# Gated DeltaNet stage of a two-layer hybrid block: exp(G) by broadcast DMA, chunk-major keys and queries, output norm with tokens on partitions, and the inverse merges of both directions in one job

## Chip, cores and metric

One core of one Trainium2 chip runs the whole program. The metric is the device time in microseconds of one execution, from the median of several runs.

## The reference, cut to what matters

The model has two layers. Each layer normalises the latent stream (1024 tokens, width 1024) and a context prefix (256 tokens), projects both through one input matrix, feeds three head groups, and projects their joined outputs back. The groups are windowed attention (8 heads of 64), a bidirectional gated DeltaNet (4 heads of 128) and a bidirectional RG-LRU. The change is almost entirely in the DeltaNet group. In the reference, for one direction:

```python
G = jnp.cumsum(g, axis=-1)
kk = jnp.einsum("bnhid,bnhjd->bnhij", k, k)
lmat = jnp.where(strict, beta[..., :, None] * jnp.exp(diff) * kk, 0.0)
a_mat = lmat + jnp.eye(C)
gam = jnp.exp(G)
w = triangular_solve(a_mat, (beta * gam)[..., None] * k)
u = triangular_solve(a_mat, beta[..., None] * v)
kdec = jnp.exp(G[..., -1:] - G)[..., None] * k
...
u_n = u_n - jnp.einsum("bhcd,bhde->bhce", w_n, s)
s_new = gl_n * s + jnp.einsum("bhcd,bhce->bhde", kdec_n, u_n)
o = einsum("bhcd,bhde->bhce", gam * q, s) + einsum("bhij,bhje->bhie", aqk, u_n)
...
rms_norm(o_forward + o_backward, norm_w) * silu(z)
```

## The kernel before

All 1280 tokens of a layer lie feature-major (features on partitions) through the projections. The matrices of the two projections are split into a high and a low part in a rounded fp32 format, so each product is three matmuls of 128x512 or 128x256. Everything else on TensorE is plain fp32, where one matmul call is two matmul records in the trace.

The program has no loops on the chip. Python threads (generators) yield operations with an engine, a cost, the buffers read and the buffers written; the class `Driver` takes the ready operation with the lowest start time plus priority and emits it. The order on every engine is thus fixed by the costs that the code states, by the tables of priorities `PR` (layer 0) and `PR1` (layer 1), and by the lists `ORDER` and `ORDER1`, which say in which order the 34 column tiles of the input projection go through TensorE. Engines run their instructions in that order.

A layer has these stages, which overlap where data allow it. `phase_a`: the input projection (`inproj`), the convolutions and norms of keys and queries (`kq_thread`, which spills them to the DRAM tensor `kqd`), the decays (`col_thread`, which leaves the running sums G in `col["G"]` and, as rows, in the tile `GR`), the matrices of each chunk (`prep_thread`, to the DRAM tensors `Md` and `Ad`), and the inverses of the 32x32 diagonal blocks (`inv_thread`, to `XXd`). `phase_b`: the recurrence. `phase_c`: attention over blocks of 128 tokens. `stage3`: the output projection and the residual.

The recurrence works in 10 chunks of 128 tokens and in two directions. For each direction and chunk `gjob` builds the 128x128 inverse of all four heads from its 32x32 diagonal blocks: `expand` on POOL (L1661), two matmul stages on 32x32 tiles of the array (`q32`, 16 records; `r32`, 24 records) and two on 64x64 tiles (`q64`, `r64`, 8 records each), with copies out of PSUM between them (L1676, L1677, L1693, L1695, L1707, L1718, L1720). `gside` loads and scales the chunk's operands: four matmuls `gb` against one-hot columns (`sel`) spread the rows of `GR` over the partitions, ACT takes the exponential (L1623), POOL multiplies keys and queries by it (L1628). `gchain` is the recurrence itself, one thread a direction: four matmuls `ks`, a subtraction on DVE (L1748), four matmuls `um`, a copy (ACT L1758, or DVE L1761), four matmuls `sm`, four state updates on DVE (L1779), and eight matmuls `om` for the output, which comes out feature-major and is summed over the directions (L1797, L1799). `gprep` lets two jobs of each direction be in flight. `gfinish` norms two chunks at a time (nine pairs in all: five in layer 0, four in layer 1): squares on ACT (L1824), one 128x512 fp32 matmul with a matrix of ones for each chunk, logarithm and exponential on ACT (L1827, L1829), a product on DVE (L1831, twice) and one with the gate (L1833).

Most DMAs are issued by SP. Attention's loads of keys (`kstd`, 8 loads) and of queries (`qstd`, 18 loads of 512 KB, into two buffers) are issued by POOL, because `q_att` is "gq".

Of the kernel before, what the change touches and what calls it, by code (L numbers as in the profile page):

```python
# [221 lines left out]
class Driver:  # L222


    def __init__(self):
# [7 lines left out]
        self.PR = {"att": -2.43, "att_k": -1.14, "att_q": 0.4, "atth": -0.23, "ba": 0.43, "evac": 0.48,  # L233
                   "gchain": 0.91, "gdn_q": -0.6, "gdn_v": 0.32, "gfin": -1.1, "gprep": 0.91, "gside": 1.4,
                   "inproj": 1.2, "inv": 0.64, "lru_x": -0.32, "lru_z": -1.34, "modlate": -1.04, "modload":
                   -3.18, "norm": 0.04, "normA": -2.69, "normB": -0.47, "normC": -0.78, "oproj": 0.17, "osplit":
                   -1.96, "prep": 0.37, "ptev": -0.1, "resid": -0.85, "rope": 1.9, "score": -0.06, "wprep":
                   -0.37, "z": -0.63}
        self.ops, self.late = [], False
        self.PR1 = {"att": -2.33, "att_k": -1.36, "att_q": -0.73, "atth": 0.31, "ba": 1.51, "evac": 0.09,  # L240
                    "gchain": 1.44, "gdn_q": -1.55, "gdn_v": 0.24, "gfin": 0.31, "gprep": 0.73, "gside": 0.54,
                    "inproj": 1.06, "inv": 0.21, "lru_x": -0.54, "lru_z": -1.12, "normA": 1.74, "normB": 2.27,
                    "normC": 6.51, "oproj": -0.33, "osplit": -2.98, "prep": -0.71, "ptev": -1.57, "resid":
                    -16.03, "rope": 5.61, "score": -0.18, "wprep": -0.07, "z": -0.78}
        self.margin, self.setpen, self.tilepen = 2.72, 1.1, 0.26
        self.cap = {"pe": 0.25, "dve": 0.3, "act": 0.33, "pool": 0.73}
# [165 lines left out]
def c_dve(n):  # L412
    return 0.07 + n / 960.0
# [14 lines left out]
def c_pool1(n):  # L428
    return 0.19 + n * 0.00097
# [99 lines left out]
class Build:  # L529
    def __init__(self, nc, tc, A, out):  # L530
# [8 lines left out]
        self.q_inv, self.q_att, self.e_rope, self.e_kq, self.e_lru = "sp", "gq", "dve", "dve", "dve"  # L539
# [445 lines left out]
    def params(self):  # L985
# [37 lines left out]
        for k in "aeflr":  # L1023
            for l in range(2):
                yield ops[k, l]

    ORDER = ("gdn_k0", "gdn_q1", "gdn_q0", "gdn_k1", "gdn_q2", "gdn_v1", "gdn_k3", "gdn_k2", "gdn_z3", "gdn_q3",
             "lru_z1", "lru_x0", "lru_x1", "lru_z0", "lru_z2", "lru_z3", "gdn_v2", "gdn_v3", "lru_x3", "gdn_v0",
             "lru_x2", "gdn_z1", "att_q3", "att_v0", "gdn_z2", "att_q0", "att_q2", "att_q1", "att_k0", "gdn_z0",
             "att_z3", "att_z0", "att_z2", "att_z1")  # L1030
    ORDER1 = ("gdn_q0", "lru_z3", "gdn_q1", "gdn_k0", "gdn_k1", "gdn_v2", "gdn_k2", "gdn_k3", "gdn_q2",
              "gdn_q3", "lru_x3", "lru_z1", "lru_x2", "lru_z0", "gdn_v3", "lru_x1", "gdn_z3", "att_v0",
              "gdn_v1", "gdn_z2", "lru_z2", "att_k0", "att_q1", "gdn_v0", "lru_x0", "att_q2", "att_z1",
              "att_q3", "att_q0", "gdn_z1", "att_z0", "gdn_z0", "att_z2", "att_z3")
# [70 lines left out]
    def zones(self):  # L1105
# [5 lines left out]
        for l in range(2):  # L1111
# [16 lines left out]
                              s=[z.slots("s", 2, [512]) for _ in range(2)], fz=z.slots("fz", 2, [1024]), osum=z.slots("osum", 10, [512]))  # L1128
# [117 lines left out]
    def col_thread(self, C):  # L1246
# [42 lines left out]
        for c0_, nck in ((0, 4), (4, 4), (8, 2)):  # L1289
# [9 lines left out]
            yield ("dve", c_dve(n), lambda: nc.vector.tensor_sub(self.GR.t[32:40, sl], pr.t[:8, :n], self.GR.t[0:8, sl].bitcast(F32)), [pr, self.GR], [self.GR])  # L1299
            pr.free()  # L1300
        C["evs"]["col"].fire()
# [280 lines left out]
    def phase_b(self, l):  # L1582
# [9 lines left out]
        for d in range(2):  # L1592
            drv.spawn(self.gprep(C, d, order[d], pre), 0.0, f"gprep{d}", self.ev(l, "gprep", d))
            drv.spawn(self.gchain(C, d, order[d]), -0.3, f"gchain{d}", self.ev(l, "gchain", d))
# [46 lines left out]
    def gjob(self, C, d, c):  # L1641
        nc, col = self.nc, self.col
        J = {}
# [610 lines left out]
```

## Time and profile before

| what | value |
|---|---|
| time, median of 3 runs | 2046.93 us (2044.83 to 2052.85) |
| time of the profiled execution | 2044.17 us |
| its span, first to last instruction | 2042.4 us |
| TensorE matmul busy | 1954.8 us, 96% |
| TensorE weight loads busy | 1551.9 us, 76% |
| VectorE (DVE) busy | 1310.4 us, 64% |
| ScalarE (ACT) busy | 1099.2 us, 54% |
| GpSimd (POOL) busy | 451.1 us, 22% |
| mean granted TensorE clock | 0.988 of full |
| moved by DMA | 327.45 MB |

The span is what the profile covers; the device time of the same execution is 1.8 us longer. The matmul row counts a matmul from its start to a modelled end, and matmuls overlap, so the distance from one start to the next is the better measure of what one costs when TensorE is full. PE is TensorE, PEld its weight loads, SP the engine that issues most DMAs.

### The profile page before, as it was taken

The page shows a single profiled execution, that of the slowest core. Times are in us where ns is not written, and L with a number is a line of the kernel's source. Part 1 is how long each engine was busy: PE and PEld are TensorE (multiplying, and loading weights), DVE is VectorE, ACT ScalarE, POOL GpSimd, SP SyncE. Part 2 cuts the span into 40 slices and gives each one's busy share as a digit, 9 for nine tenths or more (in the row PEclk, how much of TensorE's full clock was granted, in tenths as well). Part 3 has the DMA queues.
Part 4 walks back from the last instruction along what each step waited for, and adds up shares of the span by engine and source line. Part 5 has one row for each costly group of instructions (what it writes and reads, how often), then busy time and mean ns, then how long its engine had stood idle before and what let it go on. Part 6 is the DMA issues. An engine that isn't in the chain of part 4 may idle for free.

```text
span 2042.4 us, 35176 instructions
## 1 busy us (share of the span) xinstructions
PE 1954.8 (96%) x13138; PEld 1551.9 (76%) x13138; DVE 1310.4 (64%) x2529; ACT 1099.2 (54%) x1942; POOL 451.1 (22%) x630
## 2 busy tenths in 40 slices
PE   5899999999999989999999999999999999999997
PEld 2588888778888976667788787777777888766785
DVE  4867698997733455764624668888978434676523
ACT  3567667666533445565423576667657334566432
POOL 2302210000064740011322110200000676200233
PEclk8999999999999999999999999999999999999998
DMA  8125644424566796765633145643354776734644
GB/s 296 35 97 175 179 142 121 122 76 152 186 215 220 220 275 194 228 171 151 211 116 104 62 158 145 186 129 99 95 179 147 219 210 211 202 83 125 209 139 129
DMA packets 319082, 327.45 MB, mean 160 GB/s; under 512 B 62448, under 2 KB 240576, under 8 KB 318912
## 3 DMA queue, kind: packets, MB, share of 16 engines
q1 hardware_dynamic: 299040, 310.53, 49.0%
q0 software_dynamic: 19872, 14.68, 3.3%
q8 instruction: 103, 1.69, 0.4%
q14 instruction: 67, 0.55, 0.1%
HBM read 225.10 MB, written 94.79 MB: 157 GB/s over the span
## 4 chain that ended last, share of the span: by engine, by line
PE 74%; DVE 11%; ACT 6%; DMA 5%; issue 2%; SPq 1%; POOL 0%; DVEq 0%; ACTq 0%; POOLq 0%
PE psum L568 70%; PE psum L1990 3%; DVE regy L1311 2%; DVE regy L754 1%; PE psum L1199 1%; DVE regy L1470 1%; DVE regy L1318 1%; DVE regy L1472 1%; DVE regy L779 1%; DVE wlo L846 1%; DVE regy L577 1%; ACT whi L841 1%; ACT regy L1400 1%; ACT regy L1307 1%; DMA regy<-vtd 1%
## 5 line engine op out<-in xcount | busy, mean ns | idle before, releaser
L568 PE MATMUL psum<-regx,whi 128*128 128x512 f32 (+1 forms) x3328 | 952.0, 371 | 13.2 <-ACT regy L1224 6.3
L568 PEld LDWEIGHTS psum<-regx,whi 128*128 128x128 f32 x3328 | 593.3, 189 | 139.8 <-issue 19.3
L568 PE MATMUL psum<-regx,wlo 128*128 128x512 f32 (+1 forms) x1664 | 609.6, 366 | 0.9 <-DVE wlo L846 0.9
L568 PEld LDWEIGHTS psum<-regx,wlo 128*128 128x128 f32 x1664 | 314.6, 189 | 53.7 <-DVE wlo L846 1.8
L568 PE MATMUL psum<-regy,regy 128*128 128x128 f32 (+4 forms) x4064 | 321.3, 264 | 6.8 <-DVE regy L577 1.6
L568 PEld LDWEIGHTS psum<-regy,regy 128*128 128x128 f32 (+2 forms) x4064 | 263.8, 147 | 55.8 <-issue 27.3
L841 ACT ACTIVATE whi<-raw 128x1024 fp32r<-128x1024 f32 (+1 forms) x132 | 125.8, 953 | 170.6 <-PE psum L568 135.3
L568 PE MATMUL psum<-regx,regx 128*64 128x256 f32 (+2 forms) x1184 | 193.6, 365 | 10.2 <-DVE regx L1889 4.6
L846 DVE TENSOR_TENSOR wlo<-raw,whi 128x1024 fp32r<-128x1024 f32 (+1 forms) x100 | 116.2, 1163 | 78.8 <-ACT whi L841 78.1
L568 PEld LDWEIGHTS psum<-regx,regx 128*64 128x64 f32 (+1 forms) x1184 | 113.2, 162 | 63.4 <-issue 29.3
L568 PE MATMUL psum<-regy,whi 128*128 128x512 f32 (+1 forms) x576 | 155.8, 358 | 0.0
L1224 ACT ACTIVATE regy<-psum 128x512 f32<-128x512 f32 (+1 forms) x124 | 64.9, 526 | 113.7 <-PE psum L568 100.5
L1311 DVE SCALAR_TENSOR_TENSOR regy<-regy,gcv,regy 128x1282 f32<-128x1282 f32 x72 | 112.3, 1563 | 12.5 <-ACT regy L1307 11.0
L1923 ACT ACTIVATE regx<-regx,regx 128x640 f32<-128x640 f32 (+2 forms) x144 | 109.0, 760 | 18.3 <-DVE regx L1915 18.2
L2133 DVE SCALAR_TENSOR_TENSOR regy<-psum,modT,regy 128x512 f32<-128x512 f32 (+1 forms) x40 | 27.8, 696 | 137.6 <-PE psum L568 131.9
L568 PEld LDWEIGHTS psum<-regy,whi 128*128 128x128 f32 x576 | 101.4, 189 | 18.9 <-issue 3.9
L846 POOL TENSOR_TENSOR wlo<-raw,whi 128x768 fp32r<-128x768 f32 x32 | 59.2, 1850 | 243.7 <-ACT whi L841 217.8
L1409 POOL TENSOR_SCALAR_AFFINE_SELECT regy<-regy 128x512 f32<-128x512 f32 (+1 forms) x48 | 33.4, 697 | 360.4 <-ACT regy L1404 328.3
L2024 ACT ACTIVATE regx<-psum 128x512 f32<-128x512 f32 x114 | 65.1, 593 | 85.0 <-PE psum L1990 82.8
L1661 POOL TENSOR_SCALAR_AFFINE_SELECT regy<-regy 128x128 f32<-128x128 f32 (+1 forms) x240 | 70.2, 328 | 171.0 <-DMA regy<-XXd 126.2
L1628 POOL TENSOR_TENSOR regy<-regy,regy 128x512 f32<-128x512 f32 x76 | 96.7, 1288 | 50.2 <-DMA regy<-kqd 30.2
L568 PE MATMUL psum<-regy,wlo 128*128 128x512 f32 (+1 forms) x288 | 102.6, 356 | 1.6 <-POOL wlo L846 1.6
(193 smaller groups left out, 2722.5 us busy)
## 6 DMA issues: line engine op xcount, KB each, us to landing
raw<-in_win_dram SPq DMA_DIRECT2D x68, 512.0 KB
raw<-in_wout_dram SPq DMA_DIRECT2D x64, 384.0 KB
regy<-kqd SPq DMA_DIRECT2D x76, 256.0 KB
raw<-in_wmod_dram SPq DMA_DIRECT2D x32, 512.0 KB
regy<-od SPq DMA_DIRECT2D x24, 512.0 KB
regy<-ktd SPq DMA_DIRECT2D x40, 256.0 KB
regy<-vtd SPq DMA_DIRECT2D x40, 256.0 KB
regy<-Ad SPq DMA_DIRECT2D x36, 256.0 KB
```

What stands on the lines that cost most here:

```text
L568: self.nc.tensor.matmul(out, lhsT, rhs, start=start, stop=stop, skip_group_check=True)
L841: yield ("act", c_act(n), lambda: nc.scalar.activation(hi.t[:, :n], raw.t[:, :n], AF.Copy), [raw], [hi])
L846: (nc.gpsimd if e == "pool" else nc.vector).tensor_tensor(lo.t[:, :n], raw.t[:, :n], hi.t[:, :n].bitcast(F32), OP.subtract)
L1224: yield ("act", c_act(n), lambda: nc.scalar.activation(dst.t[:m, o:o + n], ps.t[:m, :n], AF.Copy), [ps], [dst])
L1311: yield ("dve", c_dve(GW), lambda: nc.vector.scalar_tensor_tensor(y.t[:, :GW], xp.t[:, k:k + GW], w[:, k:k + 1], y.t[:, :GW], OP.mult, OP. ...
L1409: yield ("pool", c_pool1(n), lambda: nc.gpsimd.affine_select(m3, s3, [[0, nch], [-1, 128]], OP.is_gt, 0.0, base=0, channel_multiplier=1), ...
L1628: yield ("pool", c_pool(512), lambda: nc.gpsimd.tensor_tensor(b.t, b.t, ga.t, OP.mult), [ga, b], [b])
L1661: nc.gpsimd.affine_select(out[:, :, 32 * b:32 * b + 32], src, [[0, 4], [0, 32]], OP.is_ge, 0.0, base=32 * b + 31 if up else -32 * b, chann ...
L1923: yield ("act:e", c_act(nk, 1) + .1, lambda: nc.scalar.activation(P, P, AF.Exp, bias=one(0, h), scale=-1.0, accum_out=one(8, h)), [Ps[j], ...
L1990: nc.tensor.transpose(pt.t[:, 128 * j:128 * j + 128], Ps[j].t[:, 128 * i:128 * i + 128], self.I.t)
L2024: yield ("act", c_act(512), lambda: nc.scalar.activation(PT.t, pt.t, AF.Copy), [pt], [PT])
L2133: yield ("dve", c_dve(n), lambda: nc.vector.scalar_tensor_tensor(xn.t[:, :n], ps.t[:, :n], g.t[:, 16 + dt, who:who + 1], xn.t[:, :n], OP.m ...
```

## The change

- `col_thread` also writes exp(G) of each token to a small DRAM tensor `egd` (10 chunks x 8 rows x 128 tokens). `gside` loads four rows of it with one DMA that repeats them on all 128 partitions, in place of the matmuls `gb` and the exponential L1623.
- `kqd` becomes chunk-major: `kq_thread` writes 512-byte pieces, and `gside` reads 2 KB in a row for each partition where it read four pieces of 512 bytes.
- One `gjob` builds the inverses of both directions of a step. Each of the four matmul stages runs once for the pair, with twice the records; the copies, loads and products are as many as before. The recurrence waits for an event `ready` that the job fires for each direction.
- `om` swaps its two operands, so that the output has tokens on partitions. `gfinish` then sums the squares over a head on DVE, takes logarithm and exponential of 8 columns, scales the output on DVE, transposes it with four matmuls against the identity for each chunk, and multiplies by the weight and the gate out of PSUM.
- Attention's loads of keys and queries are issued by ACT (`q_att` is "aq").
- The priorities `PR` and `PR1`, the numbers `margin`, `tilepen` and `cap`, and both orders of the projection's column tiles have new values.

```diff
-        self.PR = {"att": -2.43, "att_k": -1.14, "att_q": 0.4, ...
+        self.PR = {"att": -2.4, "att_k": -1.32, "att_q": -12.72, ...
...
-        self.q_inv, self.q_att, self.e_rope, self.e_kq, self.e_lru = "sp", "gq", "dve", "dve", "dve"
+        self.q_inv, self.q_att, self.e_rope, self.e_kq, self.e_lru = "sp", "aq", "dve", "dve", "dve"
...
+            b = yield ("alloc", C["prp"])
+            yield ("act:e", c_act(n), lambda: nc.scalar.activation(b.t[:8, :n], pr.t[:8, :n], AF.Exp), [pr], [b])
             pr.free()
+            yield ("sp", 32 * n, lambda: nc.sync.dma_start(
+                self.egd.t[c0_:c0_ + nck].rearrange("c p t -> p c t"), b.t[:8, :n].rearrange(...)), [b], [self.egd])
...
-        yield from self.spill(self.kqd, y, (4 if isq else 0) + h, ...)
+        for c0, n, o in ((0, 2, 0), (2, 8, 258))[1 if isq and C["last"] else 0:]:
+            yield ("sp", n << 16, lambda: nc.sync.dma_start(
+                self.kqd.t[int(isq), c0:c0 + n, :, h, :].rearrange("c p t -> p c t"),
+                y.t[:, o:o + n * 128].rearrange("p (c t) -> p c t", t=128)), [y], [self.kqd])
...
+        for i, cs in enumerate(zip(*order)):
+            for d in range(2):
+                yield ("alloc", C["lock"][d])
+            self.drv.spawn(self.gjob(C, cs), 0.02 * i, "gprep", self.ev(l, "job", i))
...
-        ps = yield ("alloc", self.ps1)
-        def gb():
-            for h in range(4):
-                self.mm(ps.t[:, 128 * h:128 * h + 128], self.sel.t[:, 4 * d + h:4 * d + h + 1].to_broadcast([128, 128]), self.GR.t[:, t0:t0 + 128], True, True)
-        yield ("pe", 0.46, gb, [self.GR], [ps])
-        yield ("act:e", c_act(512), lambda: nc.scalar.activation(ga.t, ps.t, AF.Exp), [ps], [ga])
-        ps.free()
+        yield self.load(ga.t, self.egd.t[c, 4 * d:4 * d + 4].rearrange("h t -> (h t)").partition_broadcast(128), ga, 1 << 18, R=[self.egd])
...
         def q32():
-            for h in range(4):
-                for a, b in ((0, 1), (2, 3)):
-                    self.mm(pq[sl(a), h], M[sl(b), h, sl(a)], ct[sl(b), h], True, True)
-        yield ("pe:32q", 0.25, q32, [bM, bx], [ps])
+            for d in range(2):
+                for h in range(4):
+                    for a, b in ((0, 1), (2, 3)):
+                        self.mm(pq[d][sl(a), h], M[d][sl(b), h, sl(a)], ct[d][sl(b), h], True, True)
+        yield ("pe:32q", 0.53, q32, bM + bx, [ps])
...
-                            self.mm(h4(ps)[:, h], h4(s)[:, h], h4(Q)[:, h], True, False)
-                        self.mm(h4(ps)[:, h], h4(u)[:, h], h4(aq)[:, h], s is None, True)
+                            self.mm(h4(ps)[:, h], h4(Q)[:, h], h4(s)[:, h], True, False)
+                        self.mm(h4(ps)[:, h], h4(aq)[:, h], h4(u)[:, h], s is None, True)
...
-            yield ("pe", c_pe(512, "f"), lambda: self.mm(ps.t, self.ones.t, sq.t[:, hv[i]], True, True), [sq], [ps])
+            yield ("dve", c_dve(512), lambda: nc.vector.tensor_reduce(ss.t[:, 4 * i:4 * i + 4], h4(sq.t[:, hv[i]]), AX.X, OP.add), [sq], [ss])
...
+            def tr():
+                for h in range(4):
+                    nc.tensor.transpose(ps.t[:, 128 * h:128 * h + 128], o.t[:, 128 * h:128 * h + 128], self.I.t)
+            yield ("pe", 0.44, tr, [o], [ps])
+            yield ("dve", c_dve(512), lambda: nc.vector.scalar_tensor_tensor(
+                z.t[:, hv[i]], ps.t, C["gn"].t[:, 0:1], z.t[:, hv[i]], OP.mult, OP.mult), [ps, z, C["gn"]], [z])
```

## Rows read from the trace of the kernel before

**Rows 1.** The page: span, then busy time, share and instructions of each engine.

```profile
span 2042.4 us, 35176 instructions
...
PE 1954.8 (96%) x13138; PEld 1551.9 (76%) x13138; DVE 1310.4 (64%) x2529; ACT 1099.2 (54%) x1942; POOL 451.1 (22%) x630
```

**Rows 2.** Stretches: start and end, length, busy PE, PEld, DVE, ACT, POOL, clock, DMA share, GB/s.

```profile
0.00:103.00 103.00, 72.78 (x335) 40.02 (x336) 65.05 (x114) 47.34 (x89) 31.31 (x40) 0.93 0.48 167
...
1960.00:2043.00 83.00, 68.19 (x290) 53.92 (x288) 26.29 (x32) 23.37 (x34) 25.14 (x16) 0.92 0.43 137
...
560.00:748.00 188.00, 183.90 (x2086) 159.54 (x2085) 71.77 (x170) 70.15 (x149) 110.02 (x185) 0.99 0.72 227
1586.00:1748.00 162.00, 160.05 (x1944) 139.33 (x1945) 70.01 (x170) 59.30 (x133) 111.16 (x185) 1.00 0.72 220
```

**Rows 3.** The chain that ended last: start, duration, what ran or was waited for.

```profile
680.23 4.31 DMA regy<-vtd
...
685.40 49.07 PE psum L568 x562
...
1753.80 8.66 DMA regx<-qstd
```

**Rows 4.** The state updates of layer 1 by their line: count, duration, first and last.

```profile
L1779 DVE SCALAR_TENSOR_TENSOR regy<-regy,col_gl,psum x64: 339/343/350, 1618.8 to 1747.8; 128x128 f32<-128x128 f32 x64
```

**Rows 5.** TensorE in order of time (start, duration): spreading matmuls, then recurrence matmuls.

```profile
1698.67 0.66 PE L568 MATMUL psum<-GR,sel 128*128 128x128 f32 x4
1699.17 2.00 PE L568 MATMUL psum<-regy,regy 128*128 128x128 f32 x16
1701.10 0.68 PE L568 MATMUL psum<-regy 64*64 64x64 f32 x8
```

**Rows 6.** TensorE in order of time: twenty transposes; later one chunk's sum of squares.

```profile
222.47 2.35 PE L1199 MATMUL psum<-ident,regy 128*128 128x128 f32 x20
...
612.72 1.12 PE L568 MATMUL psum<-regy,ones 128*128 128x512 f32 x2
613.77 0.61 PE L568 MATMUL psum<-regy,regy 32*32 32x32 f32 x40
```

**Rows 7.** TensorE in order of time: small-tile stages between wide matmuls, at three places.

```profile
648.61 0.39 PE L568 MATMUL psum<-regx,whi 128*128 128x512 f32 x1
648.84 0.39 PE L568 MATMUL psum<-regx,wlo 128*128 128x512 f32 x1
649.16 0.44 PE L568 MATMUL psum<-regy,regy 32*32 32x32 f32 x16
649.53 0.50 PE L568 MATMUL psum<-regx,whi 128*128 128x512 f32 x1
...
1587.80 0.40 PE L568 MATMUL psum<-regx,wlo 128*128 128x512 f32 x1
1588.12 0.68 PE L568 MATMUL psum<-regy,regy 64*64 64x64 f32 x8
1588.73 0.73 PE L568 MATMUL psum<-regx,whi 128*128 128x512 f32 x2
...
1598.85 0.40 PE L568 MATMUL psum<-regx,wlo 128*128 128x512 f32 x1
1599.18 0.96 PE L568 MATMUL psum<-regy,regy 64*64 64x64 f32 x16
1600.07 0.73 PE L568 MATMUL psum<-regx,whi 128*128 128x512 f32 x2
```

**Rows 8.** By line: ACT's exponential, and SP's issue of the key and query loads.

```profile
L1623 ACT ACTIVATE regy<-psum x40: 571/597/607, 556.1 to 1717.0; 128x512 f32<-128x512 f32 x40
...
L572 SPq DMA_DIRECT2D regy<-kqd x76: 359/402/1518, 561.3 to 1732.8; - x76
```

**Rows 9.** POOL's longest wait (total, times, longest); attention's query loads with time to landing.

```profile
POOL regx L572 <- PE psum L568: 212.2, 12, 32.0
...
regx<-qstd POOLq DMA_DIRECT2D x18, 512.0 KB, 5.1
```

More of the change, by code (lines that the diff above doesn't have):

```diff
@@ L1353, in kq_thread @@
         sq.free()
-        yield from self.spill(self.kqd, y, (4 if isq else 0) + h, ("C", "A", "B") if not (isq and C["last"]) else ("A", "B"), [])
+        for c0, n, o in ((0, 2, 0), (2, 8, 258))[1 if isq and C["last"] else 0:]:
+            yield ("sp", n << 16, lambda: nc.sync.dma_start(
+                self.kqd.t[int(isq), c0:c0 + n, :, h, :].rearrange("c p t -> p c t"),
+                y.t[:, o:o + n * 128].rearrange("p (c t) -> p c t", t=128)), [y], [self.kqd])
         tok.free()
@@ new lines, in gjob @@
+        J, sides = [{}, {}], []
+        bM, bx, bT = [], [], []
+        v4 = lambda t: t.rearrange("p (h f) -> p h f", h=4)
+        for d, c in enumerate(cs):
+            b = yield ("alloc", C["g2"])
+            yield self.load(v4(b.t)[32:128], self.chunks(self.Md, d, c, 1)[0][32:128], b, 196608, R=[self.Md])
+            bM.append(b)
+            b = yield ("alloc", C["g2"])
+            yield self.load(b.t[:, 0:256], self.XXd.t[d, c].rearrange("p k h f -> p (k h f)"), b, 1 << 17, R=[self.XXd])
+            bx.append(b)
@@ new lines, in gjob @@
+        yield ("pe:32q", 0.57, r32, bx + bM, [ps])
+        for d in range(2):
+            if d == 0:
+                ev = [(T_[0][sl(0), :, sl(1)], bT[0], 0), (T_[0][sl(2), :, sl(3)], bT[0], 2), (aux[0][sl(1), :, 0:32], bx[0], 1)]
+            else:
+                ev = [(T_[1][sl(1), :, sl(0)], bT[1], 1), (T_[1][sl(3), :, sl(2)], bT[1], 3), (aux[1][sl(2), :, 32:64], bx[1], 2)]
+            for i, (dst, bb, src) in enumerate(ev):
+                if i == 0:
+                    yield ("act", 0.18, lambda: nc.scalar.activation(dst, pr[d][sl(src)], AF.Copy), [ps], [bb])
+                else:
+                    yield ("dve", 0.2, lambda: nc.vector.tensor_copy(dst, pr[d][sl(src)]), [ps], [bb])
@@ L1727, in gjob @@
-        J["T"] = bT
-        yield ("wait", side)
-        C["jobs"][d, c] = J
+            for d in range(2):
+                for h in range(4):
+                    self.mm(pq6[d][0:64, h], M[d][64:128, h, 0:64], T_[0][64:128, h, 64:128] if d == 0 else aux[1][64:128, h], True, True)
+        yield ("pe:64q", 1.0, q64, bM + [bT[0], bx[1]], pss)
+        for d in range(2):
+            yield ("act", c_act(256), lambda: nc.scalar.activation(Q6[d][0:64], pq6[d][0:64], AF.Copy), [pss[d]], [bx[d]])
+            bM[d].free()
@@ L1731, in gchain @@
+        for d, c in enumerate(cs):
+            yield ("wait", sides[d])
+            C["jobs"][d, c] = J[d]
+            self.ev(C["l"], "ready", d, c).fire()
     def gchain(self, C, d, order):
@@ L1737, in gchain @@
             want = not (last and c < 2)
-            yield ("wait", self.ev(C["l"], "job", d, c))
+            yield ("wait", self.ev(C["l"], "ready", d, c))
             J = C["jobs"].pop((d, c))
```

201 lines of the change are left out of this document (94 added, 107 removed).

## The prediction, made before the changed kernel was run

> **What bounds the kernel now.** I read the page first: TensorE is busy for 1954.8 of 2042.4 us, so all its idle time is 87.6 us; the weight loads fill 76% [rows 1]. Then the stretches, to see where that idle time lies: 30.2 us of it in the first 103 us, while the first weights arrive, 14.8 us in the last 83, and 42.6 us in all the rest. In the two recurrence stages, 350 us together, TensorE idles for 6 us, DVE is busy for 142, ACT for 129, and the DMA engines for 72% [rows 2]. Then the chain of waits: inside the first recurrence it runs on TensorE alone for 49 us at a time, with one wait of 4.3 us for a load of values between; at the start of layer 1's attention it waits 8.7 us for a load of queries [rows 3].
>
> A busy TensorE could still be waiting on a serial recurrence, so I worked out both for one step (one chunk in each direction). In layer 1 the 64 state updates are 16 groups of four, so 15 gaps from 1618.8 to 1747.8 us: 8.6 us a group, 17.2 us a step [rows 4]. TensorE's own work in a step: 16 fp32 records take 1.93 us from start to start (0.09 of it a change of tile, below), so 0.115 each; a direction has 20 matmuls, 40 records, 4.6 us; two make 9.2 [rows 5]. The two jobs and their spreading matmuls add 2 x 2.9 us (costs below), together 15.0 of 17.2 us. The serial path of one direction is three groups of four matmuls, 2.8 us, and DVE work for which the state update is the nearest row: 4 x 0.343 = 1.4 us, and no more for each of the subtraction and the copy: 6.9 us with a little for each hand-over [rows 4, 5]. So a step has 15 us of TensorE work and some 7 us of unavoidable sequence: TensorE is the limit here, and its work is what I count.
>
> **The spreading matmuls go.** Four of them take from 1698.67 to 1699.17, 0.50 us, and 40 sets are issued: **20.0 us** off TensorE [rows 5]. ACT loses 40 exponentials of 0.597 us, 23.9 us [rows 8]; nothing waits on ACT long enough to count that.
>
> **The output norm.** One sum of squares is two records of 128x512: 1.05 us from start to start, 0.09 of it the change of tile, so 0.96; 18 of them make 17.3 us. Twenty transposes last 2.35 us, at most 0.118 each; 72 make 8.5 [rows 6]. Net **8.8 us**. DVE gets three more instructions of 512 columns in each of nine pairs. By the state update, four of which cover 512 columns, that is at most 27 x 1.4 = 37 us [rows 4], under a DVE that is free for 208 of the 350 us of the recurrences [rows 2]; without that cover it would delay only a pair's output, which the output projection needs later.
>
> **The merged inverses.** Here the number of records stays and the visits to the small tiles halve. A visit costs what lies between the wide matmuls around it, less the preceding one's own 0.23 us (648.61 to 648.84). Sixteen records on 32x32 tiles: 649.53 - 648.84 - 0.23 = 0.46 us, and the change of tile is 0.09 of that (649.16 - 648.84 - 0.23). Eight records on 64x64 tiles: 0.70; sixteen: 0.99 [rows 7]. So the second eight cost 0.29 instead of 0.70, and each of the two stages of 20 pairs saves 0.41: 16.4 us. On 32x32 tiles 40 records last 0.61 us and 16 last 0.44, 0.007 each [rows 6, 7]: a second `q32` costs 0.11 instead of 0.46, a second `r32` 0.17 instead of 0.52, 0.35 us each, 14 us over 40 stages. At most 30.4 us. At least nothing, because TensorE already shares visits: the 40 records in one visit are a `q32` and an `r32` of two jobs, and the 16 are two 64x64 stages. I take two thirds, **20 us**: most rows are single stages, some are shared. A pair has to wait for the inputs of both directions; behind it wait both recurrences' matmuls. Two pairs may be in flight, as two jobs of each direction were, and one step of lead is 17.2 us.
>
> **Loads and queues.** SP issues 40 more loads at 0.40 us, 16 us over 350 [rows 2, 8]. Reading keys and queries in one piece for each partition and writing them in four I leave at zero, since no row has the new shapes: the reads, 76 of them, should get cheaper inside the recurrence, the writes dearer before it, where they end long ahead of their use. ACT gets 26 load triggers, some 10 us at SP's price, less than half of what the exponentials gave back; POOL loses them. The wait at the start of attention was for a load from POOL's queue, 5.1 us from issue to landing in the median [rows 9]. By ACT's queue it may be shorter: between nothing and the whole 8.7 us [rows 3]; I take **3 us**, a little from each layer. `om` has as many matmuls of the same size: nothing. The exponentials for `egd` are six small ones.
>
> **The new orders and priorities** can't be priced from rows. They can't win more than the 42.6 us that TensorE idles between start and tail [rows 2], and I bound the loss by the same. I take zero.
>
> **The sum.** 20.0 + 8.8 + 20 + 3 = 51.8 us. The profiled execution took 2044.2 us, so 1992.4; the median of the runs is 2.8 us above it, so **1995 us**. The terms' own bounds (merge 0 to 30.4, attention's load 0 to 8.7) make it 1979 to 2018.
>
> **Rivals.**
>
> *Transfers become the limit of the recurrence.* The DMA engines now work for 0.72 x 350 = 252 us of it, at 220 to 227 GB/s. The broadcasts add 40 x 256 KB, 10.5 MB; at some 310 GB/s when full, 34 us. That makes 286 us, in a stage that shrinks by 47 us (all but two of the nine norm pairs' share) to 303: a share of 0.94 [rows 2]. If the engines only reach 0.9, which I choose, the stage takes 318 us, and the time is **2010 us**. For it: the chain already has a wait of 4.3 us for a load there [rows 3]. Against: the larger pieces of keys and queries. Chance 0.14.
>
> *TensorE's busy row hides gaps.* A matmul is counted to a modelled end, so part of the freed work may lie where TensorE was in fact standing still. Taking the ratio of weight-load to matmul busy time, 1551.9 / 1954.8 = 0.79 [rows 1], the 48.8 us become 39, and the time is **2005 us**. The Trainium skill (Trainium Kernel Development and Optimization, Best Practices) says to judge distance to the limit by the share of weight loads and not by that of matmuls; by that rule this rival, with 2005 us, is the base case, and no row before the change can settle it. Against it: the start-to-start distances in the rows are already what I count. Chance 0.10.
>
> *The recurrence is held by its own waits.* If the serial path is really nearer 17 us than 7, what TensorE gives up there turns into idle time: the 20, the 20 and 7 of the norm are lost, and 5 us remain: **2042 us**. For it: a pair now waits for the later of two inverses, and each inverse passes four stages with copies between them. Against: the two sums above. Chance 0.10.
>
> *ACT's queue is held by attention's loads: slower.* A trigger waits until TensorE has read the buffer that it overwrites. POOL waited 212 us for that at 12 loads, up to 32 [rows 9], with nothing behind it that mattered. Behind the trigger on ACT stand the exponentials and the copies out of PSUM that TensorE's transposes need. If each of 18 loads holds TensorE for 5.1 us, the landing time as the nearest row, that is 92 us: **2087 us**. It decides from 62 / 18 = 3.4 us a load on. The Trainium skill (TensorE: Matmul & The Clock Gate, Architectural detail: the array is 16x 32x32) says that ACT takes its instructions strictly in order; by that rule nothing on ACT can pass a waiting trigger, and the time is this rival's; the rows show such waits on POOL alone [rows 9], none on ACT. Against: the code places the trigger in ACT's order where it expects the buffer to be free, at most 2.4 us early by the priorities of attention, and ACT is idle for 46% of the span [rows 1]. Chance 0.07.
>
> *The new orders alone decide.* All of the idle time between start and tail won: **1952 us**; as much lost: **2038 us**. Chance 0.05 each.
>
> **Numbers.** The forecast itself has 0.49. About 0.5% (10 us) is what a measurement of this kernel can tell from no change, so faster is below 2037 and slower above 2057. Faster: 0.49 + 0.14 + 0.10 + 0.05 = 0.78. The recurrence held gives 0.10 of no change, and of the 0.05 of lost order 0.03 is there and 0.02 beyond: 0.13 and, with ACT's queue, 0.09. The range takes in the forecast and its bounds, both rivals that shrink the gain, and reaches to the held recurrence and the lost order: 1972 to 2040. It leaves out ACT's queue, the won order and part of the held recurrence, about 0.18.
>
> **What the profile after would show.** Right: no spreading matmul of 128x128 (160 now); matmuls with ones of 128x512 down by 36 records, 72 more transposes; small-tile runs of 32, 48 and 16 records; TensorE busy near 1908 us, with no more than 90 us idle; ACT below 1085 us. The recurrence stages, 188 and 162 us, shorter by some 20 us each, with the DMA share near 0.9 there. Wrong: gaps of TensorE behind loads in the recurrence (transfers), behind DVE or ACT (its own waits), waits on ACT ahead of the query loads with TensorE idle (ACT's queue), or idle time in the projections that was not there (the orders).

## The result and the profile after

The changed kernel takes 2027.3 us (median of 4 runs, 2023.8 to 2030.4) against 2049.2 us for the kernel before in the same session: ratio 0.989, interval 0.986 to 0.992. It is faster by 22 us, 1.1%. The forecast was 52 us less; the time lies inside the range of 1972 to 2040, near its upper end. The profiled execution took 2025.1 us.

The page after, in the same lines as [rows 1], and the stretches that answer to [rows 2] (start and end, length, busy PE, PEld, DVE, ACT, POOL, clock, DMA share, GB/s). The recurrences now reach from 560 to 843 us and from 1571 to 1766 us, to their last state updates; the last stretch lies inside the first recurrence. I had expected them some 20 us shorter each. From the first inverse to the last state update they take 336 and 195 us, where the kernel before has 247 and 168: the last updates now stand among the attention's work.

```profile
span 2023.4 us, 34895 instructions
...
PE 1927.2 (95%) x13014; PEld 1538.9 (76%) x13014; DVE 1321.9 (65%) x2556; ACT 1061.3 (52%) x1895; POOL 424.3 (21%) x604
```

```profile
0.00:103.00 103.00, 71.17 (x316) 37.86 (x316) 62.16 (x109) 41.62 (x81) 31.70 (x40) 0.87 0.45 158
560.00:843.00 283.00, 273.39 (x2723) 221.89 (x2722) 138.29 (x433) 107.56 (x251) 105.67 (x173) 0.93 0.76 247
1571.00:1766.00 195.00, 188.80 (x2157) 163.12 (x2156) 99.83 (x284) 67.72 (x163) 112.54 (x186) 0.97 0.79 252
1960.00:2024.00 64.00, 49.58 (x212) 39.28 (x210) 21.20 (x24) 17.29 (x24) 20.19 (x13) 0.90 0.42 135
...
695.00:729.00 34.00, 28.60 (x231) 22.85 (x230) 12.12 (x53) 9.94 (x28) 12.45 (x21) 0.55 0.79 272
```

The 13014 matmuls are 124 fewer than before: 160 spreading matmuls and 36 records with ones gone, 72 transposes added (a spreading matmul and a transpose leave one record each, a sum of squares two). TensorE is busy for 27.6 us less; 47 were forecast. In the recurrences its clock is granted at 0.93 and 0.97, where it was 0.99 and 1.00 [rows 2], and in one stretch of 34 us at 0.55: nine tenths of it at 1.2 GHz, the lower of the two levels, the rest at 2.4. The DMA share rose from 0.72 to 0.76 and 0.79, where I had some 0.9.

The work on small tiles answers to [rows 7] (TensorE in order of time: start, duration). The 48 records are one merged `r32`:

```profile
1591.44 0.39 PE L568 MATMUL psum<-regx,wlo 128*128 128x512 f32 x1
1591.75 0.70 PE L568 MATMUL psum<-regy,regy 32*32 32x32 f32 x48
1592.38 0.73 PE L568 MATMUL psum<-regx,whi 128*128 128x512 f32 x2
```

1592.38 - 1591.44 - 0.23 = 0.71 us for this visit; worked out in the same way for all visits, the medians are 0.47 for 24 records and 0.46 for 16 before, 0.72 for 48 and 0.72 for 32 after. The prediction's prices make it 0.69 (0.52 + 0.17) and 0.57. All visits of both traces, by this reading, with waits counted as what a visit takes beyond the shortest of its kind:

```
               visits   time    shortest of kind   waits in them
before            105   86.0 us       79.1 us          7.0 us
after              71   83.8 us       69.1 us         14.7 us   (12.6 of them in layer 0)
```

The two directions have 160 stages, but the kernel before made only 105 visits for them, so 34 visits went, not 80.

Where the stages of the program stand, worked out as the first or last start of one instruction in each trace (us): the spread into `T_` and `aux` (POOL), the exponentials of the attention (ACT), the first convolution of layer 1 (DVE), and the span's end. The lower six are from the experiments below.

```
                 first    first  last   first   first    first  last   end
                 inverse0 exp0   exp0   conv1   inverse1 exp1   exp1
before             509     759    945    1140    1580     1751   1889   2042
after              508     721    942    1141    1571     1733   1871   2023
before, 0.25       508     759    948    1142    1583     1764   1903   2048
before, 0.27       509     759    939    1147    1596     1764   1908   2059
before, 0.28       509     760    938    1145    1597     1764   1891   2065
changed, 0.25      506     719    945    1143    1582     1757   1893   2067
changed, 0.26      505     719    938    1137    1567     1744   1883   2055
changed, 0.28      506     720    949    1146    1579     1718   1849   2060
```

Layer 0 gained nothing: attention begins 37 us earlier, its exponentials end 3 us earlier, and layer 1's first convolution starts at the same time. All 19 us of the span come from layer 1: 10 of them between its first convolution and its first inverse (440 us before, 430 after), where no term of the sum lies, and 8 between its first inverse and its first exponential.

Layer 0's trouble begins where the projections that covered the inverses are used up, at 695 us (about 741 before). The chain of waits there, after (start, duration, what ran or was waited for), then ACT in order of time:

```profile
682.93 3.77 DMA regy<-kqd
...
690.08 4.86 DMA regy<-Md
...
699.09 0.60 ACT regx L679
699.74 9.30 PE psum L568 x116
709.10 0.28 ACT regy L1708
709.47 0.29 DVE regy L1710
709.79 0.29 DVE regy L1710
710.16 0.28 ACT regy L1708
```

```profile
695.41 0.38 ACTq L572 DMA_DIRECT2D regx<-qstd  x1
695.83 2.88 ACTq L572 DMA_DIRECT2D regx<-kstd  x4
698.81 0.38 ACT L1216 ACTIVATE regx<-psum 128x256 f32<-128x256 f32 x1 [3.16 <-DMA regy<-kqd]
699.09 0.59 ACT L679 ACTIVATE regx<-psum 128x512 f32<-128x512 f32 x1
```

Five triggers of attention's loads stand on ACT from 695.4 to 698.7 us, ahead of the copy of line 679, for which TensorE then waits 2.57 us (the kernel before waits 3.0 us at the same copy, behind other work of ACT):

```profile
699.74 1.87 PE L568 MATMUL psum<-sel,regx 128*128 128x2 f32 x8 [2.57 <-ACT regx L679]
```

From there on a pair's four stages run one behind another, with the copies of both directions, ACT and DVE in turn, between them. At 0.55 the 34 us hold 15 us less than they would at the full clock; how much of that is lost on the path isn't known, as no kernel was run that keeps TensorE busy there.

### The profile page after: what moved, and what is told of

The parts are those of the page before. It is cut to its first block, busy times and chain, and to the rows that moved or that the text cites. A ratio compares the mean times of both kernels' runs of the same rounds, so it can differ in the third digit from the quotient of the medians.

```text
span 2023.4 us, 34895 instructions
## 1 busy us (share of the span) xinstructions
PE 1927.2 (95%) x13014; PEld 1538.9 (76%) x13014; DVE 1321.9 (65%) x2556; ACT 1061.3 (52%) x1895; POOL 424.3 (21%) x604
## 4 chain that ended last, share of the span: by engine, by line
PE 65%; DVE 14%; ACT 8%; DMA 7%; issue 4%; SPq 1%; POOL 1%; ACTq 0%; DVEq 0%; POOLq 0%
PE psum L568 61%; PE psum L2017 3%; DVE regy L1317 3%; DVE regy L779 1%; DVE regy L577 1%; ACT regx L1950 1%; DVE regy L754 1%; DMA regy<-in_wmod_dram 1%; DVE wlo L846 1%; DVE regy L1479 1%; ACT whi L841 1%; DMA regy<-regy 1%; DVE regy L1324 1%; DVE regy L1481 1%; PE psum L1199 1%
## 5 line engine op out<-in xcount | busy, mean ns | idle before, releaser
L568 PEld LDWEIGHTS psum<-regx,regx 128*128 128x128 f32 (+1 forms) x1184 | 116.0, 166 | 56.1 <-issue 26.3
L2017 PE MATMUL psum<-ident,regx 128*128 128x128 f32 x640 | 95.4, 283 | 1.9 <-ACT regx L1950 1.3
```

The source lines that it names most:

```text
L568: self.nc.tensor.matmul(out, lhsT, rhs, start=start, stop=stop, skip_group_check=True)
L2017: nc.tensor.transpose(pt.t[:, 128 * j:128 * j + 128], Ps[j].t[:, 128 * i:128 * i + 128], self.I.t)
```

## The experiments

All 18 kernels ran beside the kernel before (2045 to 2047 us in those sessions), and the ratios are to it. "Order held" means that the planner's decisions were recorded in one kernel and replayed, so that every engine gets the same instructions in the same order but for the edit named; its lines stand ten higher than those of the kernel that it is taken from. A difference to the changed kernel is that of the two ratios (0.9893 for the changed one) times 2046 us, with some 6 us of uncertainty.

**The spreading alone, order of before held.**

```diff
-        yield ("pe", 0.46, gb, [self.GR], [ps])
-        yield ("act:e", c_act(512), ... AF.Exp), [ps], [ga])
+        yield self.load(ga.t, self.egd.t[c, 4*d:4*d+4]...partition_broadcast(128), ga, ...)
```

> The kernel before with its order of operations held, and one part of the change: exp(G) goes to DRAM in the column stage and comes back by 40 broadcast loads; the 160 spreading matmuls and 40 exponentials are gone. Theory (TensorE's work is the limit, the trace after shows these 20 us gone): TensorE loses 20 us and the time falls by 15 to 20 us, to 0.990 to 0.993 of before. Rival (the recurrence is held by its own waits, or the loads come late): the 20 us turn into idle time of TensorE, and the time is 0.997 to 1.005 of before.

2070.2 us, 1.013 [1.011, 1.015]: slower by 25 us, outside both theories. By the code the load stands where the matmuls stood, so it has no lead, and the keys' loads queue behind it on SP; the chain of waits has this (start, duration):

```profile
682.54 6.43 DMA regy<-kqd
```

In addition the first inverse starts 8 us late (517 us, 509 before), behind the new exponentials and writes. How the 25 us divide isn't worked out. An order made for matmuls is wrong for a load: this doesn't price the part.

**The output norm alone, order of before held.**

```diff
-  self.mm(ps, self.ones.t, sq) ; Ln, Exp over 1024 columns
+  tensor_reduce per token ; Ln, Exp over 8 columns ; scale ; 4 transposes per chunk
```

> The kernel before with its order of operations held, and one part of the change: the output norm with tokens on partitions (18 fewer sums of squares by ones, 72 more transposes, three more DVE instructions for each of nine pairs). Theory (TensorE's work is the limit): 17.3 - 8.5 = 8.8 us less, 0.995 to 0.997 of before. Rival (a transpose placed among other matmuls costs more than in a row, as the trace after has 17 us more in transposes): no change, 0.998 to 1.002.

2065.5 us, 1.010 [1.009, 1.012]: slower by 20 us, again outside both. Here a pair's eight transposes stand in one group, where the change has two groups of four. Between 700 and 860 us TensorE waits for DVE ahead of them three times, 1.8 us in all, so these waits aren't the 20 us there; the cause stays open, and this doesn't price the part either.

**The merged stages taken apart, order after held.** Direction 1's matmuls follow the copies of direction 0.

```diff
-        yield ("pe:32q", 0.53, q32, bM + bx, [ps])
+        yield ("pe:32q", 0.265, lambda: q32(0), ...)   # copies of 0, then:
+        yield ("~pe:32q", 0.265, lambda: q32(1), ...)
```

> The changed kernel with its order held, the merged stages taken apart again: direction 1's matmuls of each stage are issued behind the copies of direction 0, which makes 148 small-tile visits in the order of 104 (the kernel before has 167). Theory of the prediction (a visit costs 0.2 to 0.4 us of TensorE's time beyond its records, and TensorE is the limit): 44 more visits cost 12 to 18 us, 1.006 to 1.009 of the changed kernel. Rival (merging saves nothing, because the records of a stage run one behind another on one small tile and the copies between stages are waited for in both forms): within 4 us, 0.998 to 1.002.

2067.0 us, 1.011 [1.009, 1.014], 45 us slower than the changed kernel. The form has a fault that I hadn't seen: both directions use one PSUM tile, and direction 1 waits for direction 0's copies inside one visit. The trace has 103 visits by the count of the table above, 32 more than the changed kernel's 71 and not 44 more, and waits like this one (TensorE in order of time, idle time before in brackets):

```profile
1603.50 0.44 PE L578 MATMUL psum<-regy,regy 32*32 32x32 f32 x16
1604.62 0.44 PE L578 MATMUL psum<-regy,regy 32*32 32x32 f32 x16 [0.69 <-DVE regy L1702]
```

It says nothing of the price of a visit. The likely reading is that a wait of some 0.7 us in many stages costs tens of us, so that copies between stages are on the path; the added visits aren't separated from it.

**Attention's loads back on POOL, order after held.**

```diff
-        self.q_inv, self.q_att, ... = "sp", "aq", ...
+        self.q_inv, self.q_att, ... = "sp", "gq", ...
```

> The changed kernel with its order held; the 26 attention loads are triggered by POOL as before, not by ACT. Theory A (triggers on ACT hold copies that TensorE needs: 2.9 us of triggers stand ahead of the copy that TensorE waits 2.6 us for at 699.7 us, and the clock is at half from there): 3 to 12 us faster than the changed kernel, 0.994 to 0.998. Theory B (the move brings what was forecast, shorter waits for queries): 3 us slower, 1.001 to 1.004.

2044.2 us, 0.9995 [0.998, 1.001]: 21 us slower than the changed kernel, on the side of theory B but at many times its price. The chain of waits has this (start, duration):

```profile
698.03 18.23 DMA regx<-kstd
```

In this chain POOL's triggers stand behind its spread of an inverse (1.6 us), and TensorE then waits for the keys of the attention. That is only part of it: layer 1's first convolution starts 5 us later than in the changed kernel (1146 us), its first inverse 10 (1580) and its attention 17 (1750). In layer 1 the triggers stand between POOL's spreads of the inverses:

```profile
1721.89 2.25 POOL regy L1683 x6
...
1724.15 3.10 POOL regx L582 x5
1727.25 1.09 POOL regy L1683 x4
```

The expectation saw the queries only.

**Attention's loads on ACT, order of before held** (the opposite edit).

> The kernel before with its order held and one part of the change: the attention loads are triggered by ACT, not by POOL. Theory (from the run with these loads put back on POOL, 17 us slower than the changed kernel, its chain of waits held 18 us by a load on POOL's queue): 5 to 17 us faster than before, 0.992 to 0.998. Rival (only the changed kernel's order needs it, as its attention starts 38 us earlier beside the recurrence): within 4 us, 0.998 to 1.002. Rival 2 (triggers hold ACT): slower by 5 us or more.

2055.2 us, 1.004 [1.002, 1.006]: 8 us slower, by rival 2. TensorE's waits between 700 and 860 us (total, times, longest):

```profile
PE psum L578 <- ACT regx L689: 6.3, 2, 5.8
```

That is the copy of line 679 again. One of the two waits lasts 5.8 us, with four triggers of 3.35 us ahead of it on ACT, where the kernel before waits 3.0 us. Behind the triggers stands a load of ACT's function table of 1.28 us, which the kernel before has there, too. So the move is worth some 20 us to one order and costs another 8.

**The new constants and orders on the kernel before** (both tables, both orders of projections, margin and caps).

> The kernel before with the new orders, priorities, margin and caps alone. Theory (an order fits one form of the work only; taken to another it is an arbitrary one): 10 to 30 us slower, 1.005 to 1.015. Rival (the new orders carry the gain of the changed kernel): 5 to 20 us faster, 0.990 to 0.998.

2104.2 us, 1.028 [1.025, 1.032]: 58 us slower, twice what the theory said.

**One constant moved by a hundredth**, `tilepen`, three times in each kernel; the same work in other orders.

```diff
-        self.margin, self.setpen, self.tilepen = 2.72, 1.1, 0.26
+        self.margin, self.setpen, self.tilepen = 2.72, 1.1, 0.27
```

> The kernel before with one planner constant moved by a hundredth (tilepen 0.26 to 0.27), so that the same work is issued in another order. Theory (the order of before is a chosen one, and any other costs): 10 to 30 us slower, 1.005 to 1.015. Rival (orders of the same work are worth the same): within 5 us, 0.9975 to 1.0025; then the losses of the runs so far belong to their parts.

> The changed kernel with the same constant moved by a hundredth (tilepen 0.27 to 0.26). Theory (its order is a chosen one too): 10 to 30 us slower than the changed kernel, and 15 to 50 us faster than the kernel before with the moved constant, which is what the parts are worth at an equal choice of order. Rival: within 5 us of the changed kernel, 0.9975 to 1.0025.

> The kernel before with tilepen 0.25 in place of 0.26: a second other order of the same work. Both theories: slower than before, 2050 to 2075 us, as with 0.27 (2062). If it is within 5 us of before, the order of before is no special one.

> The kernel before with tilepen 0.28: a third other order. As for 0.25: 2050 to 2075 us; the three give the mean of orders that nobody chose, for the comparison with those of the changed kernel.

> The changed kernel with tilepen 0.25 in place of 0.27: a second other order. Theory A (the parts are worth what the trace counts, 19 us of TensorE's work, whatever the order): 2035 to 2050 us, so that the mean of three lies 10 to 25 us below that of the kernel before. Theory B (the parts are worth next to nothing, and the result is the choice of an order): 2050 to 2070 us, means within 8 us.

> The changed kernel with tilepen 0.28: a third other order. Theory A 2035 to 2050 us, theory B 2050 to 2070 us, as for 0.25.

```
            0.25     0.26      0.27      0.28     mean of the three moved
before     1.0026   (before)   1.0084    1.0102       1.0071
changed    1.0101   1.0064    (after)    1.0075       1.0080
```

The intervals are 0.002 to 0.003 either way. Every moved order is slower than its kernel: by 5 to 21 us before, by 35 to 43 after. The means of three differ by 2 us, so theory B held as to the whole time: between orders that nobody chose the change shows no gain at the end of the kernel. The stage table says where it goes. At attention's last exponential the four orders of the changed kernel stand at 1871, 1883, 1849 and 1893 us, a mean of 1874; the four of before at 1889, 1903, 1908 and 1891, a mean of 1898. From there on they take 152, 172, 211 and 174 us against 153, 145, 151 and 174. The last stage in two chains, first after, then with 0.26:

```profile
1884.62 123.82 PE psum L568 x536
```

```profile
1881.12 59.07 PE psum L568 x258
...
1957.81 4.25 DMA regy<-od
...
1964.41 5.30 DMA regy<-od
...
1972.08 5.46 DMA regy<-od
...
1979.94 59.70 PE psum L568 x257
```

After, the output projection runs through. With 0.26 its second half waits for the attention's last blocks, which the planner had left until then, and the two halves stand 40 us apart. With 0.25 and 0.26 layer 1's last state update starts 151 and 152 us after its first inverse, against 168 before and 195 after. This isn't the parts' doing: the kernel before reaches 149 under the new constants and 153 with the new `ORDER1` alone. The stretch tells how much other work is put into it. With 0.26 ACT holds TensorE once more (ACT, then TensorE, in order of time):

```profile
1723.02 4.56 ACTq L572 DMA_DIRECT2D regx<-kstd  x4
...
1728.99 0.64 ACT L1723 ACTIVATE regy<-psum 64x256 f32<-64x256 f32 x2
```

```profile
1722.95 1.35 PE L568 MATMUL psum<-regy,regy 64*64 64x64 f32 x16
1729.41 0.79 PE L568 MATMUL psum<-regy 64*64 64x64 f32 x5 [5.11 <-ACT regy L1723]
```

**The spreading matmuls put back as extra work, order after held.**

```diff
+        ps = yield ("alloc", self.ps1)
+        yield ("pe", 0.46, gb, [self.GR], [ps])   # nobody reads ps
+        ps.free()
```

> The changed kernel with its order held, and the 160 spreading matmuls put back as extra work (their sums go to a PSUM bank that nobody reads; exp(G) still comes by DMA). Theory A (TensorE's work sets the end, as forecast): the 20 us come back on the time, 15 to 22 us slower than the changed kernel, 1.007 to 1.011 of it. Theory B (the stages are held by other things: layer 0 by waits after its projections run out, layer 1 by the start of attention): under 8 us, below 1.004.

2041.9 us, 0.9985 [0.997, 1.000]: 19 us slower than the changed kernel by the ratios; the profiled spans, 2039.1 and 2023.4, differ by 16. Theory A. The 160 matmuls take 18.5 us from start to start, so in this order most or all of the work added to TensorE in the recurrence is on the path, in both layers: from the first inverse to layer 1's first convolution the time grows from 633 to 640 us, and from layer 1's first inverse to its last exponential from 300 to 313.

**A small matmul inside every merged stage, order after held.**

```diff
         def q32():
             for d in range(2):
+                if d:
+                    self.mm(ps.t[:, 256:258], self.I.t, self.I.t[:, 0:2], True, True)
```

> The changed kernel with its order held; between the two directions' matmuls of each of the 80 merged stages stands one small matmul on the whole array (128x2, its sum overwritten or not read), so that each visit becomes two. Theory of the prediction (0.41 us a visit, plus 0.23 us for the small matmul, TensorE the limit): 80 x 0.64 = 51 us slower than the changed kernel at most, 35 to 51 us. Rival (a visit beyond the first costs only the change of tile, 0.1 us each way, and stages that wait for copies hide it): 10 to 25 us.

2067.0 us, 1.011 [1.009, 1.013]: 44 us slower than the changed kernel, the prediction's theory. TensorE in order of time:

```profile
1596.47 0.39 PE L578 MATMUL psum<-regx,wlo 128*128 128x512 f32 x1
1596.79 0.44 PE L578 MATMUL psum<-regy,regy 32*32 32x32 f32 x16
1597.16 0.38 PE L578 MATMUL psum<-ident 128*128 128x2 f32 x2
1597.47 0.44 PE L578 MATMUL psum<-regy,regy 32*32 32x32 f32 x16
1597.84 0.73 PE L578 MATMUL psum<-regx,whi 128*128 128x512 f32 x2
```

The stage takes 1597.84 - 1596.47 - 0.23 = 1.14 us instead of 0.72, so one wedge costs 0.42 on this tile. In all, TensorE's start-to-start time for transposes, wedges and small tiles grows by 42 us. Work on TensorE counts one for one here, too.

**The new order of layer 1's projections on the kernel before.**

```diff
-    ORDER1 = ("gdn_q0", "lru_z3", "gdn_q1", "gdn_k0", "gdn_k1", "gdn_v2", "gdn_k2", ...
+    ORDER1 = ("gdn_q0", "lru_z3", "gdn_q1", "gdn_k0", "gdn_k1", "gdn_v2", "gdn_k3", ...
```

> The kernel before with the new order of layer 1's projections (ORDER1) alone. Theory (the 10 us that layer 1's preparation is shorter in all four orders of the changed kernel, first convolution to first inverse 430 to 439 us against 440 to 452, come from this order and not from the parts): that stage takes 428 to 436 us here. Rival (they come from the parts, as from the cheaper writing of keys): 440 us or more. The whole time is left open, since the end of the kernel is arranged anew: 2030 to 2060 us.

2067.6 us, 1.011 [1.009, 1.013]; the stage takes 438 us, between the two theories. With all the new constants on the kernel before it takes 434. So part of the 10 us comes from the constants and part is open; the cheaper writing of keys, which the prediction left at zero, wasn't tried alone.

**The inverses as one job for each direction again**, the rest of the change kept, planned anew; two values of `tilepen`.

```diff
-        for i, cs in enumerate(zip(*order)):  ... self.gjob(C, cs)
+        for i, c in enumerate(order):  ... self.gjob(C, d, c)
```

> The changed kernel with its inverses taken apart: one job for each direction as before, the rest of the change and the planner's constants kept, the order planned anew. To be set against the three other orders of the changed kernel (2059, 2063, 2070 us), not against the chosen one. Theory of the prediction (merging is worth 20 us of TensorE): 2075 to 2090 us. Rival (it is worth 10 us without waits, and gives back most as waits inside the visits): 2055 to 2072 us.

> The changed kernel with its inverses taken apart, as in the run before at 2097 us, with tilepen 0.26 in place of 0.27: a second order of it. Theory (merging is worth 10 to 20 us in place, in layer 0 and in layer 1's recurrence, and the rest of the 70 us is the end arranged badly): 2070 to 2095 us, with layer 0 from first inverse to layer 1's first convolution 640 to 655 us against 633. Rival (both are accidents of the order): 2050 to 2068 us, layer 0 as in the changed kernel.

2097.4 us (1.025 [1.022, 1.028]) and 2092.8 us (1.023 [1.019, 1.026]). Against the three moved orders of the changed kernel (1.0080) that is 30 to 35 us more, beyond the theory for the first and within it for the second. Layer 1's first convolution starts at 1156 and 1158 us, against 1137 to 1146, with 42 visits in layer 0 for 33. Merging is worth 10 to 20 us there under these constants, which were chosen with it: the kernel before, never merged, starts that convolution at 1140 us under its own and at 1160 under these. The rest falls after it, where the end is arranged anew.

**The old order of layer 0's projections on the changed kernel.**

> The changed kernel with the old order of layer 0's projections (ORDER) alone; priorities and the rest stay new. Layer 0 takes as long from its first inverse to layer 1's first convolution in both kernels, 632 and 633 us. Theory (the order is to blame: it uses the projections up at 695 us, and the last three pairs of inverses run uncovered, at half clock): that stretch takes 612 to 625 us here. Rival (the parts bring nothing in layer 0, whatever the order): 628 to 640 us. The whole time is left open, 2015 to 2065 us, since the end is arranged anew.

2071.6 us, 1.011 [1.008, 1.014]. From first inverse to the first convolution of layer 1 takes 606 us, but only because the first inverse starts at 541 us. Attention still starts at 721 and the convolution at 1147: nothing gained, and the measure was badly chosen. By the fixed point of the convolution it is the rival's case; the order of projections isn't what keeps layer 0 from gaining.

## Why the prediction was half right

The forecast was 52 us and the measured gain 22. Three steps failed: the price of the merged inverses, the price of the output norm, and the zero for the new orders.

**TensorE is the limit in the recurrence: right for work that is added.** Work put back there costs about its own length (two runs above), and this leaves no room for the 30 us that are missing to the rival "busy row hides gaps". That work taken away comes back in full isn't shown: the recurrences of the changed kernel became longer, and layer 0 gained nothing. In layer 0 from 695 us on the rival "held by its own waits" fits: the chain there runs through the copies of ACT and DVE. No run tests it apart from the half clock.

**The spreading matmuls, 20.0: right as TensorE's work.** They took 19.5 us from start to start, and are gone.

**The output norm, 8.8: a step that failed.** It released some 1.4 us. The sums of squares took 15.7 us from start to start, where I had 17.3. The 72 transposes take 10.6 us, where I had 8.5, and the time from the matmul ahead of a group to the group adds 7.3 us, of which 18 x 0.2 would have been there anyway. The row of the transposes (busy, mean ns, idle time before them):

```profile
L1855 PE MATMUL psum<-ident,regy 128*128 128x128 f32 x72 | 12.2, 296 | 2.8 <-DVE regy L1849 2.8
```

DVE's scaling now stands ahead of TensorE's transposes: it ended all 2.8 us of that idle time. Before, the norm's end lay behind TensorE's last part in it. The step took durations from transposes in a row; here they come in groups of four behind a wait.

**The merged inverses, 20: a step that failed.** Net 2.2 us by the table of visits. Two errors: I priced a second half at 0.11 and 0.17 us, from records 0.007 us apart, where it costs 0.26 and 0.25 (the visits above; a single `r32`, which I had at 0.52, took 0.47); and I took two thirds of what 80 saved visits would bring, though the rows already showed visits that were shared. Counting them would have given 105, and 34 saved: 10 us. Then 7.7 us came back as waits inside the visits, most of them in layer 0, where the pairs ran uncovered. The wedges show that more visits cost time in this order; the two kernels with the inverses taken apart agree, but under constants chosen for the merged form, and in layer 1 they take 156 and 150 us from the first inverse to the last state update, no more than the merged orders there.

Together the three parts took 19.5 + 1.4 + 2.2 = 23 us off TensorE, from start to start, where I had 48.8. The measured 22 us are near this, but aren't shown to come of it: half of the parts' work lies in layer 0, which gained nothing, and 10 us of the gain lie where no part does.

**Attention's loads by ACT, 3: mis-sized in both directions.** The changed kernel would lose some 20 us without it, the kernel before loses 8 by it. The rival of ACT's queue is real, too: copies that TensorE needed stood behind the triggers, with waits of 2.6 us (after), 5.1 us (0.26) and 5.8 us (before with the loads on ACT; 3.0 us without them), but at the four loads of keys in a layer and not at each of 18. The strict order that the Trainium skill gives for ACT (TensorE: Matmul & The Clock Gate, Architectural detail: the array is 16x 32x32) agrees with these rows.

**The new orders, zero: the step that failed most.** I bounded them by TensorE's idle time, 42.6 us either way. On the kernel before they cost 58, and a hundredth in one constant costs 5 to 43. The measured 22 us can be laid out so, by the ratios: the new constants on the old work, +58; then the other parts at those constants, -80, of which 41 remain if the three moved orders stand for the changed kernel (1.0282 to 1.0080), and 38 are the choice of its order (1.0080 to 0.9893). Each of these rests on one to three orders. The moved orders of both kernels, each under its own constants, say otherwise: there the parts and the new constants together bring nothing (2 us the other way), and the 22 us are the choice of the order, which puts the changed kernel 38 us ahead of its moved ones and the kernel before 15. So that the time fell into the range is luck as much as the parts, and what the parts are worth by themselves, 0 to 41 us by these two readings, isn't decided. No run has the changed kernel under all the old constants.

**Transfers as the limit: no.** The share was 0.76 and 0.79 over the recurrences, where the rival had 0.94; in a stretch with more, 0.88 from 1571 to 1600 us, TensorE was busy for 28.8 of 29 us. And extra matmuls at the same transfers cost time.

What stays open: what makes layer 1's preparation 10 us shorter, what the parts are worth apart from the order, how much the half clock after 695 us costs, and whether an order exists in which layer 0 gains as well.

## What to carry to other kernels

Before pricing a merged stage, count how often the trace already runs two of them together, and price the second half by a row of the merged shape or by the nearest whole stage, not by the spacing of its last records. Where a planner or a hand-made order stands behind both kernels, run each with its order shaken two or three times: the spread, here 20 to 40 us, is the uncertainty of any claim on a part, and a part tried in an order made without it can look harmful when it is not. A trigger for a large load on an engine's queue is an instruction with a price of its own: look what copy stands behind it.

## What the runs showed of the hardware

Four triggers of attention's key loads kept ACT for 2.9 us after, 3.4 us in the kernel before with the loads on ACT, and 4.6 us with 0.26. Single ones took from 0.33 to 2.97 us (the longest with 0.26, at 1723.7 us), where a trigger of a query load took 0.37 to 0.45 in these three traces.

The clock of TensorE fell where small-tile visits with waits between them had replaced the wide matmuls, in every order of the changed kernel: granted at 0.61 to 0.71 from 695 to 730 us in the three moved ones, while the kernel before has 1.00 there, still under its projections. The rows with 0.26 and of the kernel before, columns as above:

```profile
695.00:730.00 35.00, 27.99 (x252) 23.28 (x253) 13.55 (x57) 12.15 (x33) 10.38 (x13) 0.71 0.82 289
...
695.00:730.00 35.00, 35.00 (x420) 30.61 (x420) 16.57 (x40) 14.92 (x32) 22.33 (x38) 1.00 0.68 211
```

So this fall belongs to the changed kernel or to its constants and not to one unlucky order. It isn't the merging alone: with the inverses taken apart the clock is at 0.66 from 730 to 765 us. Where the kernel before runs out of projections it falls as well, but less, to 0.91 from 741 to 780 us.
